# The stepwise inversion of 16x16 diagonal blocks in VectorE's queue instead of GpSimd's, in a two-model forward pass

## The chip, the cores and the metric
The kernel runs on one core of a Trainium2 chip. Its time is the device time of that core in microseconds (us). Before the change it is 3070.37 us, the median of 3 runs (3067.53 to 3080.65). Engines are named as the profile names them: PE is TensorE's matrix multiply, PEld its weight load, DVE is VectorE, ACT is ScalarE, POOL is GpSimd, SP is SyncE, whose queue (SPq) issues most DMAs.

## The reference, cut to what matters
Two networks run one after the other on 512 tokens of width 1024. The first has two layers, and each layer has two gated feed-forward blocks around a mixing block. The mixing block joins three mixers: attention over selected keys (8 heads), an RWKV-7 recurrence (4 heads) and a gated delta rule (4 heads). The second network has one layer with two more mixers, cross attention and a mixture of 16 experts; the change does not touch it.

RWKV-7 and the gated delta rule are both solved in chunks of 64 tokens. Each chunk needs the solution of a unit lower triangular system:

```
lower = where(strict, einsum('bhncd,bhnsd->bhncs', kb, k) * decay, 0.0)
sol = triangular_solve(eye(C) + lower, rhs, left_side=True, lower=True, unit_diagonal=True)
```

The kernel computes the result of both recurrences with the same code, which it calls the delta mixers. For each block of 128 tokens (two chunks, 8 heads in all) it inverts the 16x16 blocks on the diagonal of these systems exactly, in 15 steps of elimination, and treats what lies outside these blocks by three rounds of substitution with matrix products.

## The kernel before, in words
**Stages.** In each of the two layers of the first network there is a stage, here the delta stage, in which the attention of the layer and both delta mixers run interleaved. It works on four blocks of 128 tokens, numbered 0 to 3. For one block the work is:
- `rwkv_front` and `gdn_front` (from line 1132, `delta_fronts`) make products on TensorE and write the system's matrix into a tile `low` (name in the code: `L`). The last TensorE instructions for it are four transposes of the tile `gsq`, in the rows `bank<-consts,gsq`, and ScalarE copies them into `low`.
- `delta_inverses` (line 672) sends the 16x16 diagonal blocks of `low` through DRAM into the tile `LL` of 64 rows, 8 DMAs out (`lows<-low`) and one back (`LL<-lows`). POOL masks `low` (one instruction, `low<-low,consts`). Then come the steps: in step j a product of two broadcast views is written into a scratch third of `LL` and subtracted from the inverse, which is another third; 15 steps of two instructions, each 64 rows by 15 to 64 elements. One DMA takes the inverse out (`inverses<-LL`), and 8 bring it into the tile `DD` (`DD<-inverses`). The two tiles `DD0` and `DD1` take turns.
- `delta_solve` (line 704) begins with TensorE products of `DD` and `low`, then of the right-hand sides, for RWKV (`rrh`) and for the gated delta rule (`grh`), and then makes the rounds of substitution (`Y`).
- `delta_states` carries the states `S` through the chunks, and `dsa_attend` makes the attention's scores (`kz,qT`), softmax (`sm`) and values (`po`), also in four blocks, of growing length.

A block's front may be built when the fronts before it are done and the solves are no more than two blocks back.

**What sets the order.** The streams above are Python generators. `weave` (line 310) advances one of them at a time, the first whose operands are ready. Whether they are ready is told by a ledger in the program: `account` (line 2192) enters each instruction with a cost from a small table and keeps a clock for each engine:

```
if self.name == "POOL":
    return n * 2.1 + 220
return n / 0.96 + (200 if any(isinstance(x, bass.AP) for x in args[2:3]) and len(args) == 4 or "accum_out" in kw else 150)
```

The last line is VectorE's. When no stream is ready, the time until the next one is, in this ledger, is filled with small matmuls of a constant, `bank<-mean`, one for 234 ns (line 262):

```
n, self.idle = int(self.idle / 234), 0.0
for _ in range(n):
    self.t.matmul(p[:, :128], self.mean, self.mean, start=True, stop=True)
```

They compute nothing that is used; in this text they are called fillers. Afterwards a scheduler of the framework sets the order in each engine's own queue. Each engine then executes its queue strictly in that order and waits at semaphores. All engine instructions pass through the helper at line 2184, so the profile shows that line for nearly all of them, and they are told apart by the names of their tiles.

Of the kernel before, what the change touches and what calls it, by code (L numbers as in the profile page):

```python
# [14 lines left out]
OP = mybir.AluOpType  # L15
# [185 lines left out]
class Net:  # L201
# [470 lines left out]
    def delta_inverses(self, pool, l, f):  # L672

        g = self.g
        DD = [self.tl(pool, [128, 8, 128], f"DD{i}", 1) for i in range(2)]
        for d in DD:
            g.memset(d, 0.0)
        for b in range(NB):
            yield lambda: min(f["front"]) > b and min(f["back"]) > b - 2  # L680
            L, D, low, inv = f["L", b], DD[b % 2], self.lows[l * NB + b], self.inverses[l * NB + b]
            for k in range(8):
                at = slice(16 * k, 16 * k + 16)
                self.move(low[k].rearrange("q s t -> s q t"), L[at, :, at])
            W = self.tl(pool, [64, 3, 256], "LL", 1)
            g.memset(W[:, 1], 0.0)
            g.memset(W[:, 1, ::17], 1.0)
            self.move(W[:, 0], low.rearrange("k q s t -> (k q) (s t)"))

            N, X, t = (W[:, i].rearrange("p (i c) -> p i c", i=16) for i in range(3))  # L690
            for j in range(15):
                c, n = j + 1, 15 - j
                g.tensor_tensor(t[:, :c, :n], N[:, None, j + 1:, j].to_broadcast([64, c, n]),
                                X[:, :c, j, None].to_broadcast([64, c, n]), op=OP.mult)
                g.tensor_tensor(X[:, :c, j + 1:], X[:, :c, j + 1:], t[:, :c, :n], op=OP.subtract)
            self.move(inv.rearrange("k q s t -> (k q) (s t)"), W[:, 1])
            for k in range(8):
                at = slice(16 * k, 16 * k + 16)
                self.move(D[at, :, at], inv[k].rearrange("q s t -> s q t"))
            g.tensor_tensor(L, L, self.c("off16")[:, None, :].to_broadcast([128, 8, 128]), op=OP.mult)  # L700
            f["DD", b] = D
            f["D"] = b + 1
# [1654 lines left out]
```

## Time and profile before
| | |
|---|---|
| median of 3 runs | 3070.37 us |
| profiled execution, its own time | 3068.61 us |
| its span, first to last instruction | 3066.7 us |
| mean granted TensorE clock | 0.982 |
| PE busy / DVE busy / ACT busy / POOL busy | 2967.5 / 1779.5 / 1314.9 / 491.1 us |
| delta stage, first layer, from its first product with `DD` to its end | 614.16 to 764.90 us |
| the same in the second layer | 1776.6 to 1929.0 us |

The kernel is bound by TensorE nearly everywhere. The chip's profile counts an engine busy while an instruction is in it; fillers count as busy too. The time that an engine stood still before an instruction is told in square brackets behind a row, with the instruction or DMA that ended the wait. Names are those of the program's tiles, with buffer numbers left out in the trace and kept in the order below.

### The profile page before, as it was taken

Reading aid. Unit: us, or ns where it says so; the run is one execution under the profiler, and the core shown is the slowest. Engines: PE = TensorE matmul, PEld = TensorE weight load, DVE = VectorE, ACT = ScalarE, POOL = GpSimd, SP = SyncE. Lnnn points to the kernel's source line nnn. Section 1 sums busy time; section 2 is a strip of 40 time slices with the busy share of each in tenths; the row PEclk is TensorE's granted clock in tenths of the full one; section 3 lists DMA queues with packets and bytes.
Section 4 is the critical chain, followed back from the end, with each engine's and each line's share of the span. In section 5 each row is a group of like instructions: output and inputs, shape, how many; then the busy total and the mean of one; then the engine's idle time right before and its main releaser. Section 6 shows DMA issues by size and latency. Waiting matters only on the chain. (4 is left out here: it accounts for less than half of the span.)

```text
span 3066.7 us, 40239 instructions
## 1 busy us (share of the span) xinstructions
PE 2967.5 (97%) x15422; PEld 2366.7 (77%) x15422; DVE 1779.5 (58%) x2969; ACT 1314.9 (43%) x2117; POOL 491.1 (16%) x674
## 2 busy tenths in 40 slices
PE   9999999999999999999998999999999999989997
PEld 7888866786888888888866786888887777767775
DVE  5343559574544445444559675543445657649988
ACT  3222444544322234222344445422225455558886
POOL 1000144431000000000044431000001000026532
PEclk9999999999999999999999899999999999999999
DMA  4333322001333333333322000333333312759993
GB/s 133 100 96 100 120 76 76 18 15 33 108 98 96 96 91 102 96 96 96 119 83 72 24 17 14 124 97 97 99 94 114 99 49 63 289 172 375 388 385 142
DMA packets 129529, 349.95 MB, mean 114 GB/s; under 512 B 30400, under 2 KB 37456, under 8 KB 129200
## 3 DMA queue, kind: packets, MB, share of 16 engines
q1 hardware_dynamic: 120608, 325.17, 32.4%
q0 software_dynamic: 3648, 12.85, 1.3%
q10 hardware_dynamic: 5072, 9.27, 0.8%
q8 instruction: 123, 2.02, 0.3%
q14 instruction: 78, 0.64, 0.1%
HBM read 325.28 MB, written 21.95 MB: 113 GB/s over the span
## 5 line engine op out<-in xcount | busy, mean ns | idle before, releaser
L2184 ACT ACTIVATE wh<-w 128x1024 fp32r<-128x1024 f32 (+2 forms) x386 | 400.1, 1037 | 1115.4 <-PE bank L2184 790.7
L2184 PE MATMUL bank<-hh,wl 128*128 128x512 f32 x2000 | 783.5, 392 | 16.7 <-POOL wl L2184 9.7
L2184 PE MATMUL bank<-hh,wh 128*128 128x512 f32 x2000 | 790.5, 396 | 0.7 <-ACT hh L2184 0.6
L2184 PE MATMUL bank<-hl,wh 128*128 128x512 f32 x2000 | 782.5, 391 | 3.2 <-DVE hl L2184 3.1
L2184 PEld LDWEIGHTS bank<-hh,wl 128*128 128x128 f32 x2000 | 377.2, 189 | 101.8 <-POOL wl L2184 14.1
L2184 PEld LDWEIGHTS bank<-hh,wh 128*128 128x128 f32 x2000 | 376.8, 188 | 91.4 <-issue 13.0
L2184 PEld LDWEIGHTS bank<-hl,wh 128*128 128x128 f32 x2000 | 377.2, 189 | 86.4 <-DVE hl L2184 6.8
L2184 DVE TENSOR_TENSOR wl<-w,wh 128x1024 fp32r<-128x1024 f32 (+1 forms) x334 | 399.5, 1197 | 74.1 <-ACT wh L2184 57.3
L2184 PE MATMUL bank<-ul,wh 128*128 128x512 f32 x704 | 274.3, 390 | 0.0
L2184 PE MATMUL bank<-uh,wl 128*128 128x512 f32 x704 | 273.9, 389 | 0.0
L2184 PE MATMUL bank<-uh,wh 128*128 128x512 f32 x704 | 273.2, 389 | 0.0
L2184 DVE TENSOR_TENSOR hl<-w,hh 128x1024 fp32r<-128x1024 f32 x192 | 238.3, 1265 | 21.2 <-ACT hh L2184 15.1
L2184 DVE TENSOR_TENSOR u<-bank,rfeat 128x512 f32<-128x512 f32 x88 | 60.8, 691 | 279.0 <-PE bank L2184 279.0
L2184 ACT ACTIVATE hh<-w 128x1024 fp32r<-128x1024 f32 x192 | 201.4, 1059 | 45.0 <-PE bank L2184 45.0
L2184 DVE SCALAR_TENSOR_TENSOR x<-bank,x 128x512 f32<-128x512 f32 x96 | 66.4, 692 | 241.2 <-PE bank L2184 241.2
L2184 POOL COPY cosi<-consts 128x128 f32<-128x128 f32 x4 | 2.2, 557 | 1079.5 <-ACT sg L2184 1079.5
L2184 DVE TENSOR_TENSOR g<-bank,rfeat 128x512 f32<-128x512 f32 x88 | 60.9, 692 | 186.6 <-PE bank L2184 185.8
L2184 PEld LDWEIGHTS bank<-ul,wh 128*128 128x128 f32 x704 | 132.2, 188 | 28.7 <-DVE ul L2184 1.3
L2184 PEld LDWEIGHTS bank<-uh,wh 128*128 128x128 f32 x704 | 132.2, 188 | 27.4
L2184 PEld LDWEIGHTS bank<-uh,wl 128*128 128x128 f32 x704 | 132.2, 188 | 27.2
L2184 POOL TENSOR_TENSOR wl<-w,wh 128x1024 fp32r<-128x1024 f32 (+1 forms) x52 | 122.1, 2348 | 186.3 <-ACT wh L2184 176.0
L2184 PE MATMUL bank<-hh,exh 128*96 128x512 f32 (+1 forms) x272 | 109.3, 403 | 0.0
(574 smaller groups left out, 4619.4 us busy)
## 6 DMA issues: line engine op xcount, KB each, us to landing
w<-in_wgu SPq DMA_DIRECT2D x176, 512.0 KB, 3.5
w<-in_wd SPq DMA_DIRECT2D x64, 512.0 KB, 3.6
w<-in_w_eg SPq DMA_DIRECT2D x64, 512.0 KB, 6.8
w<-in_w_eu SPq DMA_DIRECT2D x64, 512.0 KB, 6.3
w<-in_w_ed SPq DMA_DIRECT2D x62, 512.0 KB, 8.2
w<-in_wd SPq DMA_DIRECT2D x32, 384.0 KB, 3.1
w<-in_w_o SPq DMA_DIRECT2D x20, 512.0 KB, 4.1
w<-in_w_gd SPq DMA_DIRECT2D x16, 512.0 KB, 3.5
```

The costliest lines, as they stand in the source:

```text
L2184: r = f(*args, **kw)
```

## The change
Two lines of the loop over the 15 steps name another engine: `self.v`, VectorE, where `g`, POOL, stood. The clearing of the tiles and the mask of `low` stay on POOL. The formulas and the tiles are the same.

```
             for j in range(15):
                 c, n = j + 1, 15 - j
-                g.tensor_tensor(t[:, :c, :n], N[:, None, j + 1:, j].to_broadcast([64, c, n]),
-                                X[:, :c, j, None].to_broadcast([64, c, n]), op=OP.mult)
-                g.tensor_tensor(X[:, :c, j + 1:], X[:, :c, j + 1:], t[:, :c, :n], op=OP.subtract)
+                self.v.tensor_tensor(t[:, :c, :n], N[:, None, j + 1:, j].to_broadcast([64, c, n]),
+                                     X[:, :c, j, None].to_broadcast([64, c, n]), op=OP.mult)
+                self.v.tensor_tensor(X[:, :c, j + 1:], X[:, :c, j + 1:], t[:, :c, :n], op=OP.subtract)
             self.move(inv.rearrange("k q s t -> (k q) (s t)"), W[:, 1])
```

Since the ledger charges the steps to VectorE, the order of instructions changes too, in the two delta stages and nowhere else. TensorE, first layer, where the fillers stand ahead of block 1's products (- is before, + is now; `kz` and `qT` are attention, `rE2` belongs to RWKV):

```order
 L2184 MATMUL bank_793_4442<-kz_439_2583,qT_432_2576 128x128
 L2184 MATMUL bank_794_4443<-kz_439_2583,qT_432_2576 128x128
-L2184 MATMUL bank_799_4454<-mean_67 128x128 x6
+L2184 MATMUL bank_799_4454<-mean_67 128x128 x31
 L2184 MATMUL bank_799_4454<-rE2_745_4280,consts_8_100 128x256
```

There were 6 fillers and there are 31. In the whole stage of one layer there were 59 and there are 118.

TensorE a little further on, before: the products of block 1's matrix, then its transposes to tokens, and in the last row the transposes of `gsq`, which complete block 1's `low`.

```order
L2184 MATMUL bank_804_4473<-rE0_744_4279,rkk_747_4282 128x128 x2
L2184 MATMUL bank_804_4473<-rR_425_2569,rE0_744_4279 128x128 x2
L2184 MATMUL bank_805_4480<-rkk_747_4282,rcs_743_4278 128x128 x2
L2184 MATMUL bank_805_4480<-rR_425_2569,rcs_743_4278 128x128 x2
L2184 MATMUL bank_806_4487<-rkk_747_4282,rcs_743_4278 128x128 x2
L2184 MATMUL bank_806_4487<-rR_425_2569,rcs_743_4278 128x128 x2
L2184 MATMUL bank_808_4495<-consts_8_100,rV_426_2570 128x128 x2
L2184 MATMUL bank_808_4495<-consts_8_100,rkk_747_4282 128x128 x2
L2184 MATMUL bank_809_4502<-consts_8_100,rE3_746_4281 128x128 x2
L2184 MATMUL bank_809_4502<-consts_8_100,rA_424_2568 128x128 x2
L2184 MATMUL bank_810_4509<-consts_8_100,gsq_775_4378 128x128 x4
```

TensorE at the same place now (`DD0_716` holds block 0's inverse, `low_720` is block 0's matrix; the first two products with `DD0_716` stand just ahead of these):

```order
L2184 MATMUL bank_810_4532<-consts_8_100,rV_426_2570 128x128 x2
L2184 MATMUL bank_810_4532<-consts_8_100,rkk_747_4282 128x128 x2
L2184 MATMUL bank_811_4539<-DD0_716_4130,low_720_4138 128x128 x4
L2184 MATMUL bank_812_4545<-grh_736_4207,DD0_716_4130 128x128 x4
L2184 MATMUL bank_813_4551<-consts_8_100,rE3_746_4281 128x128 x2
L2184 MATMUL bank_813_4551<-consts_8_100,rA_424_2568 128x128 x2
L2184 MATMUL bank_814_4558<-rrh_728_4170,low_720_4138 128x128 x4
L2184 MATMUL bank_815_4564<-grh_736_4207,low_720_4138 128x128 x4
L2184 MATMUL bank_816_4570<-rV_426_2570,ak_800_4488 128x64 x4
L2184 MATMUL bank_817_4576<-Y0_738_4216,low_720_4138 128x128 x4
L2184 MATMUL bank_818_4582<-Y1_742_4277,low_720_4138 128x128 x4
L2184 MATMUL bank_819_4588<-consts_8_100,gsq_775_4378 128x128 x4
```

Before, the transposes of `gsq_775` stood 19 rows ahead of the first product with block 0's inverse; now they stand 13 rows behind it. Block 2's moved in the same way behind block 1's inverse; block 3's stood behind block 2's inverse already.

VectorE, block 1 of the first layer, before: preparing block 2's RWKV operands, one for one with the decay tile `DT` of the gated delta rule.

```order
L2184 TENSOR_TENSOR rE3_820_4590<-rK_422_2566,rE3_820_4590 128x256
L2184 SCALAR_TENSOR_TENSOR DT_847_4681<-bank_848_4682,gb_479_2776,consts1_9_102 128x128
L2184 TENSOR_TENSOR rK_422_2566<-rK_422_2566,cols_63 128x2x128
L2184 SCALAR_TENSOR_TENSOR DT_847_4681<-bank_848_4682,gb_479_2776,consts1_9_102 128x128
L2184 TENSOR_TENSOR rE2_819_4589<-rR_425_2569,rK_422_2566 128x256
```

VectorE at the same place now, with the steps of block 1 (`LL_820`) between:

```order
L2184 SCALAR_TENSOR_TENSOR DT_839_4719<-bank_840_4720,gb_479_2776,consts1_9_102 128x128
L2184 TENSOR_TENSOR LL_820_4603<-LL_820_4603 64x15
L2184 TENSOR_TENSOR rE2_825_4661<-rR_425_2569,rK_422_2566 128x256
L2184 TENSOR_TENSOR LL_820_4603<-LL_820_4603 64x15
L2184 SCALAR_TENSOR_TENSOR DT_839_4719<-bank_840_4720,gb_479_2776,consts1_9_102 128x128
L2184 TENSOR_TENSOR LL_820_4603<-LL_820_4603 64x2x14
L2184 TENSOR_TENSOR rR_425_2569<-rR_425_2569,rW_423_2567 128x2x128
L2184 TENSOR_TENSOR LL_820_4603<-LL_820_4603 64x2x14
```

Each of the 30 instructions of a block's chain needs the one before it. Between them stand other instructions: 21 in block 0, 29 in block 1, 30 in block 2 and 5 in block 3 (an instruction and the read of its accumulator counted as one).

## Rows read from the trace of the kernel before
**Rows 1.** The page: busy us, share of the span, instructions.
```profile
PE 2967.5 (97%) x15422; PEld 2366.7 (77%) x15422; DVE 1779.5 (58%) x2969; ACT 1314.9 (43%) x2117; POOL 491.1 (16%) x674
```
**Rows 2.** Stretches of the delta stage; first layer, then all of the second.
```profile
core 0: us, PE busy (x) PEld busy (x) DVE busy (x) ACT busy (x) POOL busy (x), PEclk, DMA share, GB/s
614.16:639.43 25.27, 23.91 (x204) 21.18 (x205) 21.88 (x57) 13.43 (x35) 12.87 (x33) 1.00 0.08 12
639.43:665.91 26.48, 26.35 (x275) 22.80 (x275) 18.97 (x58) 8.91 (x20) 12.32 (x33) 0.94 0.10 16
665.91:718.13 52.22, 47.23 (x530) 36.76 (x529) 29.94 (x92) 25.79 (x69) 12.14 (x32) 0.97 0.09 24
718.13:764.90 46.77, 44.96 (x400) 35.82 (x400) 20.40 (x50) 21.83 (x48) 0.00 (x0) 0.88 0.08 24
1776.60:1929.00 152.40, 143.47 (x1410) 117.58 (x1411) 91.28 (x255) 71.26 (x173) 37.23 (x98) 0.94 0.09 22
```
**Rows 3.** Timeline of TensorE, first layer: start, us, operation, count, [idle before <-releaser].
```profile
584.80 0.61 PE L2184 MATMUL bank<-consts,gsq 128*128 128x128 f32 x4
...
614.16 1.13 PE L2184 MATMUL bank<-DD,low 128*128 128x128 f32 x8 [0.70 <-DMA lows<-low]
...
639.43 1.40 PE L2184 MATMUL bank<-DD,low 128*128 128x128 f32 x8 [1.27 <-DMA DD<-inverses]
...
665.91 1.06 PE L2184 MATMUL bank<-DD,low 128*128 128x128 f32 x8
...
718.13 2.05 PE L2184 MATMUL bank<-DD,low 128*128 128x128 f32 x8 [4.55 <-DMA DD<-inverses]
719.97 1.92 PE L2184 MATMUL bank<-rrh,DD 128*128 128x128 f32 x8
...
761.53 3.62 PE L2184 MATMUL bank<-mean 128*128 128x128 f32 x30
```
**Rows 4.** Timeline of POOL, first layer: the mask and the steps, blocks 0 and 1.
```profile
591.93 2.35 POOL L2184 TENSOR_TENSOR low<-low,consts 128x1024 f32<-128x1024 f32 x1 [18.63 <-ACT PT L2184]
594.25 12.46 POOL L2184 TENSOR_TENSOR LL<-LL 64x15 f32<-64x15 f32 x30
...
619.81 12.38 POOL L2184 TENSOR_TENSOR LL<-LL 64x15 f32<-64x15 f32 x30
```
**Rows 5.** Timeline of SyncE's DMA queue, first layer, blocks 0 and 1.
```profile
586.06 4.36 SPq L668 DMA_DIRECT2D lows<-low  x8
...
612.46 3.68 SPq L668 DMA_DIRECT2D lows<-low  x8
```
**Rows 6.** Timeline of VectorE, first layer.
```profile
577.22 1.12 DVE L2184 SCALAR_TENSOR_TENSOR DT<-bank,gb,consts 128x128 f32<-128x128 f32 x4
...
586.17 0.16 DVE L2184 COPY wc<-rW 128x4 f32<-128x4 f32 x1
586.24 0.35 DVE L2184 CUSTOM_DVE_ANT_0 sm<-bank,consts,ssq 128x128 f32<-128x128 f32 x1
...
592.07 2.50 DVE L2184 TENSOR_TENSOR rkk<-rkk,rcs 128x256 f32<-128x256 f32 x1
...
596.17 0.47 DVE L2184 TENSOR_TENSOR rcs<-rK,rE 128x256 f32<-128x256 f32 x1
...
624.72 0.74 DVE L2184 SCALAR_TENSOR_TENSOR rb<-bank,consts 128x256 f32<-128x256 f32 x2
```
**Rows 7.** VectorE's groups by form, small shapes: count | busy us, mean ns of one.
```profile
L2184 DVE SCALAR_TENSOR_TENSOR gsp<-gsp,gsp 128x16 f32<-128x16 f32 x18 | 3.2, 175 | 0.6
L2184 DVE TENSOR_TENSOR M<-oe,oe 128x64 f32<-128x64 f32 x1 | 0.2, 218 | 0.0
```

## The prediction
> **What bounds the kernel now.** I read the busy table of the page first. TensorE is busy for 97% of the span, VectorE for 58%, GpSimd (POOL) for 16% [rows 1]. So time is won or lost where TensorE waits, or where it does something that is no work. Next I read TensorE's timeline inside the delta stage of a layer, which is the only place where the order of instructions differs between the two kernels. In it I looked for the four places at which TensorE first multiplies with an inverted block, `bank<-DD,low`: 614.16, 639.43, 665.91 and 718.13 us [rows 3]. These four points and the stage's end, where the output projection starts at 764.90, cut the stage into four stretches of 25.27, 26.48, 52.22 and 46.77 us [rows 2]. In the second layer the same five points span 152.40 us, against 150.7 in the first [rows 2], so one layer is worked out and doubled. TensorE waits 0.70 us before the first point, 1.27 before the second, nothing before the third, and 4.55 before the fourth [rows 3].
>
> What paces the first three points is a loop through several queues. When TensorE has made the last half of a block's matrix (the transposes `bank<-consts,gsq`), ScalarE copies it, and SyncE sends 8 DMAs (`lows<-low`) and one back. POOL then does the 30 steps, SyncE sends the inverse out and 8 DMAs back into `DD`, and TensorE can go on. The pieces: from the transposes at 584.80 [rows 3] to the first DMA at 586.06 [rows 5] 1.3 us; from the first DMA at 612.46 [rows 5] to the first step at 619.81 [rows 4] 7.4 us; 30 steps 12.4 us [rows 4]; from the end of the steps (594.25 + 12.46 = 606.71) [rows 4] to the product at 614.16 [rows 3] 7.45 us. The loop therefore costs 28.5 us per block, and 12.4 of them are the step that is moved. Before the change it hardly shows: in TensorE's queue the transposes of blocks 1 and 2 stand ahead of the previous block's `DD`, so two blocks are on the way at once.
>
> **The change, part by part.** Removed from POOL: 240 instructions, 30 in each of 8 blocks, 12.4 us a block [rows 4]. That in itself is worth nothing, since POOL waits for most of the stage. The mask of the matrix stays on POOL: 2.35 us at 591.93 [rows 4], and a VectorE instruction that falls into it still takes 2.50 us instead of 0.4 [rows 6].
>
> Added to VectorE: the same 240. The trace before has no VectorE step of this form, so I bound it. From above: 0.175 us with 16 elements and 0.218 with 64 [rows 7], 0.2 on average, if each step is charged whole; 30 make 6 us. From below: a 4-element copy is followed by the next start after 0.07 us (586.17 to 586.24) [rows 6]; 30 make 2.1 us. Where a step stands between other instructions I take 0.12 us, 3.6 us a block, since it has 15 to 64 elements and a 128-element instruction starts 0.26 us after its neighbour (four in 1.12 us) [rows 6]. Where steps follow each other I take 0.2.
>
> But the steps do not stand alone. In VectorE's order the chains of blocks 0, 1 and 2 alternate with other instructions, one for one: 21, 29 and 30 of them. Those start 0.33 us apart with 256 elements [rows 6], 0.26 with 128, and I take 0.6 with 512. So block 1's chain lasts 15 x 0.33 + 10 x 0.26 + 4 x 0.25 + 3.6 = 12.2 us, with waits for TensorE some 13; block 2's 21 x 0.33 + 4 x 0.6 + 4 x 0.26 + 3.6 = 14. Block 0's starts behind the instruction at 596.17 [rows 6], lasts 16 x 0.33 + 4 x 0.26 + 3.6 = 10, and near its end waits for a product behind the long row of filler matmuls; it ends near 607.7, a us later than on POOL. Only block 3 has five others, 7 us. So in three of four blocks the loop gets nothing shorter.
>
> The second effect weighs more: TensorE's order changes, because the ledger that writes it charges the steps to another engine. (1) The filler matmuls (`bank<-mean`) in the stage go from 59 to 118 per layer. Thirty records, that is 15 fillers, take 3.62 us [rows 3], 0.24 each, so 59 more cost 14.2 us of TensorE. (2) The transposes of blocks 1 and 2 now stand behind the previous block's `DD`, so the loop can no longer run ahead. (3) Attention's third block moves behind the last `DD`.
>
> To price the stretches I counted the columns streamed in each, a transpose's as half: before, 13,568, 14,592, 28,672 and 22,720; now 18,432, 13,760, 21,696 and 30,336. The stretches of before, less their waits (0.7 in the last, estimated) and less 0.24 us for each of the 0, 0, 6 and 27 fillers, come to 24.0, 26.5, 46.2 and 39.6 us: 1.71 ns a column. Fillers are now 0, 0, 30 and 42.
>
> Sum for one layer:
> - To the first `DD`: its chain ends 1 us later, +1.0. TensorE waits there with 10 us of work queued behind, which moves into later stretches.
> - First to second `DD`: 5,120 columns to the transposes (8.8 us), a slow start after the wait 1.0, then 1.3 + 7.4 + 13 + 7.45 = 39.0; TensorE's own 31.5 fit inside. Against 25.3: +13.7.
> - Second to third: 3,072 columns (5.3), 1.0 + 1.3 + 7.4 + 14 + 7.45 = 36.5. Against 26.5: +10.0.
> - Third to fourth: TensorE is longer, 37.1 for its columns, 7.2 for 30 fillers and 1.0 = 45.3; the loop ends at 19.0 + 1.0 + 1.3 + 7.4 + 7 + 7.45 = 43.2. Against 52.2: -6.9.
> - Fourth to the end: 51.9 + 42 x 0.24 + 1.0 = 63.0. Against 46.8: +16.2.
>
> Together +34.0 us, twice +68.0. The slow start is an estimate: after the wait of 4.55 us the first two groups took 2.05 and 1.92 us [rows 3], where the same group took 1.06 at 665.91 [rows 3], and the granted clock of that last stretch is 0.88, a mean of its two levels of 1.2 and 2.4 GHz [rows 2]; so it costs up to 1.9 us, and I take half. The profiled execution took 3068.61 us, 1.9 beyond its span and 1.8 below the median of the runs. 3068.6 + 68.0 = 3136.6; I say 3136.
>
> What queues behind the added waits: VectorE's queue blocks at the first step of each block until its DMA has landed, with the operands of TensorE's next products behind it; TensorE waits for `DD` with all else behind it.
>
> On how the steps add up, the row shows 256-element instructions of 0.41 us starting 0.33 apart (two in 0.74) [rows 6]. The Trainium skill (VectorE: DVE Perf Modes, "The DRAIN you can't avoid") says that the next instruction does not start until the pipe is empty, and advises to keep the number of instructions low; this speaks against 240 small ones on the busier engine. By it block 1's chain would be about 3.6 us longer and the time some 3150; by the row the overlap is there, and the sum goes by the row.
>
> **The rivals.**
> *Faster: only the steps count.* The chain of 30 runs on VectorE in 6 us instead of 12.4, so each loop is 6 us shorter, and the waits before `DD` (0.70 + 1.27 + 4.55 = 6.5 us) [rows 3] go, with 1.9 of slow start: -8.4 a layer, 3052 us. For it: 0.2 us a step against 0.41 on POOL [rows 4, 7]. Against it: the alternation and the order of TensorE. It decides if block 1's first step starts before 622 us of the span instead of near 634. The Trainium skill (GPSIMD Engine Reference, section 4.1) has this rule: two-input elementwise work belongs on VectorE, GpSimd being about twice slower; the rows agree on one step alone. Chance 0.04.
> *Fillers only.* All waits at `DD` are hidden: the stretches cost 31.5, 23.5, 44.3 and 62.0 us, together +10.5 a layer, 3090 us. For it: nothing that the trace shows hides 7 to 13 us there. Against it: the loop without its steps alone is 16 us. Chance 0.12.
> *Heavier.* The interleaved instructions wait for TensorE in turn, and the chains of blocks 1 and 2 take 6 us more each: +12 a layer, 3160 us. For it: many of them read a `bank`. Against it: those products are mostly done when the chain starts late. Chance 0.20.
> *No change*, since the transfers and not the steps pace the loop: 3070 us, chance 0.04.
>
> **How the numbers follow.** My forecast holds 0.60. The range reaches from the fillers-only case to the heavier one: 3091 to 3160 us. A measurement of this kernel tells 0.5%, 15 us, from no change. Slower by more than that are the forecast, the heavier case and most of fillers-only: 0.89. Within it lie the no-change case and a remainder of fillers-only: 0.07. Faster: 0.04.
>
> **What would show it.** TensorE's waits for `DMA DD<-inverses` should be 4 to 7, 5 to 9 and 10 to 15 us before the first three `DD` of a layer and near none before the fourth, the reverse of before. The stage should last some 34 us longer per layer, the rest of the span the same. VectorE's busy time should grow by 25 to 48 us, POOL's fall by about 99. The chain on VectorE should last 10 to 16 us in blocks 0 to 2 and 7 in block 3. I am wrong if the first step of block 1 starts as early as before, or if TensorE stands still less in the stage than it does now.

## The result, and the profile after

The changed kernel takes 3146.47 us (median of 4 runs, 3145.57 to 3150.33), the kernel before 3068.95 (4 runs). The ratio is 1.0259, with a 95% interval of 1.0238 to 1.028. The forecast was 3136 us in a range of 3091 to 3160. The profiled execution took 3147.16 us with a span of 3145.4: 78.7 us more than the span of before. The busy table of the changed kernel, against [rows 1]:

```profile
PE 3005.5 (96%) x15658; PEld 2409.1 (77%) x15658; DVE 1820.0 (58%) x3209; ACT 1316.8 (42%) x2117; POOL 414.9 (13%) x434
```

VectorE's busy time grew by 40.5 us and POOL's fell by 76.2. Next the stretches of the delta stage, cut at the same four products as in [rows 2]; the last row is the second layer from its first product with `DD` to the stage's end. The columns are those of [rows 2].

```profile
615.03:662.70 47.67, 39.86 (x336) 34.29 (x337) 29.08 (x97) 15.77 (x41) 2.96 (x3) 0.75 0.04 7
662.70:706.42 43.72, 30.91 (x198) 26.97 (x198) 26.90 (x91) 14.62 (x38) 2.76 (x3) 0.73 0.08 19
706.42:751.85 45.43, 41.99 (x497) 36.35 (x498) 26.29 (x95) 17.01 (x44) 2.87 (x2) 0.94 0.09 19
751.85:807.85 56.00, 55.40 (x514) 44.48 (x515) 26.94 (x72) 31.32 (x76) 0.00 (x0) 0.97 0.08 23
...
1815.81:2006.36 190.55, 167.25 (x1545) 141.51 (x1545) 110.24 (x356) 80.19 (x201) 9.09 (x8) 0.86 0.08 18
```

The first two stretches grew by 22.4 and 17.2 us, the third shrank by 6.8, the last grew by 9.2; together 42.1. TensorE's granted clock in the first two is 0.75 and 0.73, where it was 1.00 and 0.94. TensorE's timeline of the first layer shows the places that [rows 3] show of before:

```profile
598.44 7.16 PE L2184 MATMUL bank<-mean 128*128 128x128 f32 x62 [0.80 <-DVE LL L2184]
...
615.03 2.04 PE L2184 MATMUL bank<-DD,low 128*128 128x128 f32 x8 [6.25 <-DMA DD<-inverses]
...
626.37 0.60 PE L2184 MATMUL bank<-consts,gsq 128*128 128x128 f32 x4
...
662.70 2.05 PE L2184 MATMUL bank<-DD,low 128*128 128x128 f32 x8 [5.66 <-DMA DD<-inverses]
...
670.48 0.61 PE L2184 MATMUL bank<-consts,gsq 128*128 128x128 f32 x4
...
706.42 2.05 PE L2184 MATMUL bank<-DD,low 128*128 128x128 f32 x8 [9.83 <-DMA DD<-inverses]
...
726.42 0.61 PE L2184 MATMUL bank<-consts,gsq 128*128 128x128 f32 x4
...
751.85 1.13 PE L2184 MATMUL bank<-DD,low 128*128 128x128 f32 x8 [3.43 <-DMA DD<-inverses]
```

The `gsq` rows are the transposes that complete a block's matrix; they now follow the previous block's product, and the next product waits for the inverse. What the loop consists of is seen for block 1 first in SyncE's DMA queue, which answers to [rows 5]:

```profile
627.63 3.63 SPq L668 DMA_DIRECT2D lows<-low  x8
632.49 0.47 SPq L668 DMA_DIRECT2D LL<-lows  x1
654.33 0.46 SPq L668 DMA_DIRECT2D inverses<-LL  x1
657.45 3.62 SPq L668 DMA_DIRECT2D DD<-inverses  x8
```

VectorE's timeline between these DMAs:

```profile
632.83 2.58 DVE L2184 SCALAR_TENSOR_TENSOR gQ<-gQ,gsq 128x256 f32<-128x256 f32 x1
...
637.93 0.16 DVE L2184 TENSOR_TENSOR LL<-LL 64x15 f32<-64x15 f32 x1
638.01 0.41 DVE L2184 TENSOR_TENSOR rE<-rR,rK 128x256 f32<-128x256 f32 x1
638.35 0.16 DVE L2184 TENSOR_TENSOR LL<-LL 64x15 f32<-64x15 f32 x1
...
646.28 0.42 DVE L2184 SCALAR_TENSOR_TENSOR ak<-bank,consts 128x256 f32<-128x256 f32 x1 [0.98 <-PE bank L2184]
...
654.08 0.17 DVE L2184 TENSOR_TENSOR LL<-LL 64x15 f32<-64x15 f32 x1
```

The first step starts 10.3 us behind the first DMA, because VectorE has other work in front of it. The chain then takes 16.3 us, since every second instruction is another one, and some of those wait for TensorE or ScalarE.

### The profile page after: what moved, and what is told of

It is laid out like the page before. It is cut to its first block, busy times and chain, and to the rows that moved or that the text cites. A ratio compares the mean times of both kernels' runs of the same rounds, so it can differ in the third digit from the quotient of the medians.

```text
span 3145.4 us, 40718 instructions
## 1 busy us (share of the span) xinstructions
PE 3005.5 (96%) x15658; PEld 2409.1 (77%) x15658; DVE 1820.0 (58%) x3209; ACT 1316.8 (42%) x2117; POOL 414.9 (13%) x434
## 5 line engine op out<-in xcount | busy, mean ns | idle before, releaser
L2184 ACT ACTIVATE hh<-w 128x1024 fp32r<-128x1024 f32 x192 | 201.3, 1059 | 45.3 <-PE bank L2184 45.1
```

The source lines that it names most:

```text
L2184: r = f(*args, **kw)
```

## The experiments

All ratios are to the kernel before, run on the same chip beside them.

**Order and engine apart.** The helper runs a step on one engine and books it on another in the ledger, so the four combinations can be had. In e1 the steps run on VectorE and TensorE keeps its order of before; in e2 they run on POOL and TensorE has the order of after.

```
+def _step(does, pays):
+    def call(*args, **kw):
+        does.eng.tensor_tensor(*args, **kw)
+        pays.account(args, kw, list(args))
...
-                self.v.tensor_tensor(X[:, :c, j + 1:], X[:, :c, j + 1:], t[:, :c, :n], op=OP.subtract)
+                _step(self.v, self.g)(X[:, :c, j + 1:], X[:, :c, j + 1:], t[:, :c, :n], op=OP.subtract)
```

(e1; in e2 it is `_step(self.g, self.v)`, and the product of each step is edited alike.)

> The 240 steps run on VectorE, but the ledger books them on POOL, so TensorE keeps the order of before (59 fillers per layer, the transposes of blocks 1 and 2 ahead of the previous block's first product with DD). Theory A, the order costs: 3060 to 3085 us, because VectorE's interleaved chains end about when POOL's did and nothing is put behind them on TensorE; waits of TensorE for the inverses at the first three points under 4 us each. Theory B, the engine costs (VectorE's queue is blocked by the steps and the steps by the queue): 3110 to 3150 us, with waits of 4 us and more at the first three points.

> The 240 steps run on POOL as before, but the ledger books them on VectorE, so TensorE has the order of after (118 fillers per layer, the transposes behind). Theory A: 3120 to 3140 us, a little under after, since POOL's chain starts as soon as its DMA has landed (7.4 us behind the first DMA instead of 10.3) and lasts 12.4 us instead of 16; the second and third stretch about 40 and 37 us instead of 47.7 and 43.7. Theory B: 3070 to 3090 us.

Measured: e1 3100.85 us, ratio 1.0101 (1.0077 to 1.0124); e2 3118.12 us, 1.0172 (1.0147 to 1.0197). Neither theory alone holds: e1 lies between its two ranges, e2 2 us below the first of its own. The engine costs 1.0%, the order 1.7%, and their sum, 2.7%, is about the 2.6% of the change.

In e1 little of the cost is a late inverse. TensorE's waits for the inverse in the first layer's stage of before, from 584 to 765 us: us in total, times, longest.

```profile
PE bank L2184 <- DMA DD<-inverses: 5.8, 2, 4.5
```

The same of e1, from 584 to 778 us:

```profile
PE bank L2184 <- DMA DD<-inverses: 8.5, 2, 6.5
```

That is 2.7 us of the 12.3 by which e1's stage is longer, from the first transposes to its end. TensorE's other waits grew by 4.6 us, and its rows took 5.0 more, with the granted clock at 0.93 where it was 0.95. In e2 the steps are back on POOL. TensorE's timeline still shows waits for the inverse: smaller ones than after's at the first three products, a larger one at the fourth.

```profile
612.73 2.04 PE L2184 MATMUL bank<-DD,low 128*128 128x128 f32 x8 [5.72 <-DMA DD<-inverses]
...
654.95 1.05 PE L2184 MATMUL bank<-DD,low 128*128 128x128 f32 x8
...
689.37 1.74 PE L2184 MATMUL bank<-DD,low 128*128 128x128 f32 x8 [3.72 <-DMA DD<-inverses]
...
736.48 2.04 PE L2184 MATMUL bank<-DD,low 128*128 128x128 f32 x8 [6.24 <-DMA DD<-inverses]
```

**The fillers.** e3 is the kernel after, with the stage's fillers booked in the ledger and not issued.

```
-            self.t.matmul(p[:, :128], self.mean, self.mean, start=True, stop=True)
+            (_ledger_only(self.t) if getattr(self, "mute", 0) else self.t.matmul)(p[:, :128], self.mean, self.mean, start=True, stop=True)
```

> The kernel after, with the same ledger, but the 118 fillers per layer of the delta stage booked and not issued. If every filler costs its 0.24 us: 28 us a layer less, about 3090 us. If only those cost that stand where TensorE does not wait soon after (the last stretch, 43 of them): 10 us a layer less, about 3126 us. If they only keep the clock up: no less than 3146 us, with a lower granted clock.

Measured: 3158.92 us, ratio 1.0303 (1.0278 to 1.0327), 12 us slower than with them: the third case of the expectation. The intervals of the two ratios just touch, but the fastest of the four executions of e3 (3157.50) is slower than the slowest of after (3150.33). The kernel after, up to its first product with `DD`:

```profile
560.00:615.03 55.03, 46.29 (x359) 40.67 (x359) 43.58 (x140) 23.53 (x64) 13.18 (x17) 0.92 0.04 6
```

Four stretches of e3: up to the first product, the last two of the first layer's stage, and 60 us behind the second layer's stage.

```profile
560.00:616.43 56.43, 41.66 (x267) 34.87 (x266) 42.27 (x140) 23.26 (x64) 13.21 (x17) 0.71 0.04 6
...
704.79:755.23 50.44, 37.98 (x438) 31.25 (x438) 26.55 (x95) 17.14 (x44) 2.52 (x2) 0.84 0.08 17
755.23:808.91 53.68, 48.60 (x430) 36.25 (x431) 26.27 (x72) 30.99 (x76) 0.00 (x0) 0.94 0.03 10
...
2011.47:2071.47 60.00, 58.53 (x243) 47.48 (x243) 31.91 (x41) 21.37 (x27) 0.00 (x0) 0.95 0.42 141
```

The granted clock fell from 0.92 to 0.71 ahead of the first product and from 0.94 to 0.84 in the third stretch, which got 5 us longer. The last stretch lost 42 fillers, 10 us by their duration, and got only 2.3 us shorter: without them TensorE stands still for 5.1 us there (0.6 with them), and the granted clock is 0.94 instead of 0.97. Of the 12 us, some 5 lie in the two stages. Another 6.9 lie behind the second one, where both kernels have the same instructions: the granted clock of the last row, 0.95, is 1.00 in the 60 us behind that stage of after.

**The transposes' place.** e9 is the kernel after, but a solve of block 0 or 1 waits in the program for the next block's front.

```
-        yield lambda: f["D"] > b
+        yield lambda: f["D"] > b and (b > 1 or min(f["front"]) > b + 1)
```

> As after, but the solve of blocks 0 and 1 waits in the program until the next block's front is built, so the transposes of blocks 1 and 2 stand ahead of the previous block's first product with DD again, as before the change; the steps still alternate on VectorE and the ledger still books them there (the row of 31 fillers stays). If the transposes' place is what the new order costs: 3095 to 3110 us, the level of e1. If the fillers or the place of attention's third block cost: 3125 to 3150 us.

Measured: 3093.31 us, ratio 1.0073 (1.0057 to 1.0088), 53 us less than after and 2 us below the first range of the expectation, with the row of 31 fillers still there. TensorE's timeline of e9; the wait for the inverse before the second product is gone:

```profile
609.18 0.60 PE L2184 MATMUL bank<-consts,gsq 128*128 128x128 f32 x4
614.66 1.37 PE L2184 MATMUL bank<-DD,low 128*128 128x128 f32 x8 [2.79 <-DMA lows<-low]
...
649.13 0.46 PE L2184 MATMUL bank<-DD,low 128*128 128x128 f32 x2 [0.24 <-ACT low L2184]
```

The edit moves more than the transposes: the scores of attention's second block and part of those of its third stand further ahead too. But of the 29.9 us by which e9's first stage is shorter than that of after, 23.0 lie ahead of the third product, and attention's third block stands behind that product in both.

**The alternation on VectorE.** e5 is e1, and e7 is the kernel after, with the steps of a block together in VectorE's queue: an instruction traced behind them goes behind the last step if the ledger has it start no earlier than the first (SHIFT = 0).

```
+def _behind(eng, ins, start):
+    if getattr(eng, "last", None) is not None and eng.net.together and start >= eng.first + SHIFT:
+        eng.net.tc.add_manual_dep(ins, eng.last.name, mybir.DependencyInfo(
+            mybir.DependencyClass.NoSync, mybir.DependencyReason.DATA), reason="steps together")
```

> As e1 (steps on VectorE, order of before on TensorE), but the 30 steps of a block stand together in VectorE's queue: what is traced behind them, and is not due earlier by the ledger, is queued behind the last step. Theory I, the alternation is what makes VectorE dear: the chain falls from 13 to 18 us to 6 to 7, the first three points come no later than before, the wait before the fourth falls under 2 us: 3045 to 3068 us. Theory Q, the queue behind the steps is what costs (TensorE waits for operands that VectorE now makes 6 us later): 3080 to 3100 us, with TensorE waiting for VectorE's tiles.

> As after (ledger and TensorE's order), but the 30 steps of a block stand together in VectorE's queue. Theory I: the loop gets about 9 us shorter in blocks 1 and 2, stretches of 38 and 35 us instead of 47.7 and 43.7; 3100 to 3118 us, no more than e2. Theory Q: 3135 to 3150 us.

Measured: e5 3097.17 us, ratio 1.009 (1.0075 to 1.0106), no measurable gain over e1 and in the range of theory Q; e7 3131.82 us, 1.0207 (1.0192 to 1.0223), 15 us less than after and between its two ranges. Theory I falls for the order of before: the chain is indeed down to 7.4 us, and TensorE waits for no inverse, but for other tiles of VectorE instead. Block 0's chain in VectorE's timeline of e5 (line 2363 is the helper's):

```profile
594.14 7.40 DVE L2363 TENSOR_TENSOR LL<-LL 64x15 f32<-64x15 f32 x30 [2.01 <-DMA LL<-lows]
```

TensorE's waits in e5 from 585 to 785 us: who waits for what, us in total, times, longest.

```profile
PE bank L2184 <- DVE S L2184: 7.0, 2, 6.8
PE bank L2184 <- DVE gqk L2184: 5.7, 1, 5.7
PE bank L2184 <- DVE rE L2184: 5.2, 2, 4.6
PE bank L2184 <- DVE Y L2184: 4.6, 1, 4.6
```

In e7 TensorE waits for no inverse in this stage either, but for 24 us for three tiles of VectorE; the longest, in the same columns:

```profile
PE bank L2184 <- DVE mn L2184: 10.6, 2, 8.0
```

So a block's steps cost VectorE's queue time that TensorE sees in one form or the other. Together they make other operands late. Alternating they make the inverse late in the order of after, and in the order of before (e1) both, other operands more than the inverse.

**The last block alone.** In e4, e6 and e13 only block 3's steps are on VectorE, in TensorE's order of before: alternating, together, and together behind what is due within 1 us of the first step.

```
-                g.tensor_tensor(X[:, :c, j + 1:], X[:, :c, j + 1:], t[:, :c, :n], op=OP.subtract)
+                _step(self.v if b == 3 else g, g)(X[:, :c, j + 1:], X[:, :c, j + 1:], t[:, :c, :n], op=OP.subtract)
```

(e4; e6 and e13 have `_behind` besides, with a SHIFT of 0 and of 1000 ns.)

> Only block 3's steps run on VectorE, the ledger books all on POOL, TensorE's order is that of before row for row. If the steps of the last block bind there: its chain falls from 11.9 to about 7 us, the wait of 4.55 us before the fourth product goes together with up to 1.9 us of slow start: 4.5 to 6.4 us a layer, 3056 to 3060 us. If VectorE's queue holds the chain up: 3066 to 3072 us, with the wait still there.

> As e4 (only block 3 on VectorE), but its 30 steps stand together in VectorE's queue. Theory I: the chain falls from 12.3 us (e4) to 6 to 7, the wait of 6.4 us before the fourth product goes and 1.9 us of slow start with it: 3053 to 3062 us. Theory Q: attention's instructions, 6 us later, take the place of the wait: 3066 to 3076 us.

> As e6 (block 3's steps together on VectorE, the rest on POOL), but the instructions that the ledger has due up to 1 us behind the first step go ahead of it, the recurrence's state S among them, for which TensorE waited 6.9 us in e6. If VectorE's queue has room there: 3050 to 3060 us. If the softmax instructions that now stand behind the steps make the next wait: 3062 to 3070 us, with TensorE waiting some 5 us for sm.

Measured: e4 3072.80 us, ratio 1.0022 (1.0008 to 1.0036), slightly slower; e6 3063.92, 0.9991 (0.9981 to 1.0001); e13 3063.82, 0.9989 (0.9977 to 1.0). Neither e6 nor e13 can be told from the kernel before. In e4 the chain starts behind softmax work and alternates with it, and in TensorE's timeline the wait before the fourth product grew from 4.55 us [rows 3] (the profiled execution took 3083.05 us, the longest of twelve):

```profile
720.26 2.05 PE L2184 MATMUL bank<-DD,low 128*128 128x128 f32 x8 [6.44 <-DMA DD<-inverses]
```

In e6 that wait is gone, and one for the state S stands in its place. TensorE's longest wait of e6 in the first layer's stage:

```profile
PE bank L2184 <- DVE S L2184: 7.1, 2, 6.9
```

In e13 the longest is one for Y, where the expectation had `sm`:

```profile
PE bank L2184 <- DVE Y L2184: 4.8, 1, 4.8
```

**Steps on POOL, booked dearer.** If the order counts, the ledger can make a better one. In the kernel before, each step is booked at 413, 700 and 800 ns.

```
-        n = max(int(np.prod(x.shape[1:])) for x in aps)
+        n = max(int(np.prod(x.shape[1:])) for x in aps) if not getattr(self, "fixed", 0) else (self.fixed - 220) / 2.1
...
+        pays.fixed = 413
+        pays.account(args, kw, list(args))
```

(e10; 700 in e11 and 800 in e12.)

> The kernel before, steps on POOL, but the ledger books each step at the 413 ns that POOL takes for it (12.4 us for 30) instead of by its formula (some 260 to 350). In the order that comes of it block 2's transposes stand 27 rows behind block 1's first product with DD; block 1's stand ahead as before. If the transposes' place is what an order costs: TensorE waits 5 to 10 us before the third point and none more before the second; 3085 to 3105 us. If a truer ledger makes a better order: 3050 to 3068 us.

> As the last, but each step booked at 700 ns, far above what it takes: all transposes stand ahead of the previous block's first product, block 3's too (38 rows ahead of block 2's), and 30 fillers per layer are left of 59. If the transposes' place decides: no wait for the inverses over 1 us at any of the four points, 3045 to 3062 us. If fillers are needed for the clock: a granted clock under 0.975 and 3066 to 3085 us.

> As the last, each step booked at 800 ns: block 3's transposes stand 55 rows ahead of block 2's first product, and a dozen fillers per layer are left in the stage. The transposes' place: 3045 to 3062 us, as the kernel booked at 700. The clock: slower than that one by 5 to 20 us, with a granted clock lower by 0.003 or more.

Measured: e10 3058.57 us, ratio 0.9971 (0.9956 to 0.9985); e11 3058.99, 0.9971 (0.9959 to 0.9982); e12 3052.22, 0.9946 (0.9928 to 0.9964). e12 beats both kernels, and all three beat the one before. For e10 my expectation was wrong in sign: block 2's transposes do stand behind block 1's product, and the kernel is faster. I had counted rows; its timeline counts time:

```profile
640.39 1.13 PE L2184 MATMUL bank<-DD,low 128*128 128x128 f32 x8 [2.56 <-DMA DD<-inverses]
...
653.13 0.60 PE L2184 MATMUL bank<-consts,gsq 128*128 128x128 f32 x4
...
690.68 1.16 PE L2184 MATMUL bank<-DD,low 128*128 128x128 f32 x8
```

Between block 2's transposes and its product TensorE had 37.6 us of other rows, 3.6 of them a wait for VectorE, and no wait for the inverse. e12 goes further, 59.5 us for block 2 and 48.9 for block 3, with no wait for an inverse in the whole stage:

```profile
643.97 0.60 PE L2184 MATMUL bank<-consts,gsq 128*128 128x128 f32 x4
...
686.32 0.60 PE L2184 MATMUL bank<-consts,gsq 128*128 128x128 f32 x4
...
703.50 1.16 PE L2184 MATMUL bank<-DD,low 128*128 128x128 f32 x8
...
735.25 1.16 PE L2184 MATMUL bank<-DD,low 128*128 128x128 f32 x8
```

e11 has no wait for an inverse in its two stages either. It keeps 55 of the 60 fillers that the trace of before has in the first stage from its first transposes on, so little of the 8.8 us that it gains can be theirs. In the two stages of before TensorE waited 11.4 us for the inverse. e12 keeps 35, 9 of 34 behind the first product, and its clock hardly suffered: 0.981 over the whole run, 0.982 before. No run tells how much of its lead over e11 comes from the fewer fillers.

So the rule that these runs fit is not "transposes ahead" but: TensorE waits for the inverse by what the loop takes beyond the time that its own rows fill between a block's transposes and that block's product. In the first layer, us from transposes to product, with the wait for the inverse in it:

| | block 1 | block 2 | block 3 |
|---|---|---|---|
| before | 34.2, wait 1.3 | 33.4, none | 28.9, wait 4.6 |
| after | 36.3, wait 5.7 | 35.9, wait 9.8 | 25.4, wait 3.4 |
| e1 (VectorE, order of before) | 38.0, none | 38.3, none | 31.6, wait 6.5 |
| e2 (POOL, order of after) | 30.7, none | 29.2, wait 3.7 | 28.2, wait 6.2 |
| e9 (VectorE, solve held back) | 40.0, none | 35.4, none | 27.2, wait 4.4 |
| e12 (POOL, booked at 800) | 64.9, none | 59.5, none | 48.9, none |

Where TensorE waited, the time in the table is the loop's own. Where it did not, the loop can be read to the end of the eight `DD<-inverses`, and some 1.4 to 1.9 us more, which the rows with a wait show from there to the product: 27 to 38 us, less than the table's time in each of these blocks.

Before the change, block 1's loop took 34.2 us and not the 28.5 of the prediction. Its first DMA, at 612.46 [rows 5], came 7.2 us behind the transposes instead of 1.3: in SyncE's queue it stands right behind the DMAs that bring block 0's inverse.

```profile
608.72 3.64 SPq L668 DMA_DIRECT2D DD<-inverses  x8
```

So two blocks on the way at once hold each other up in that queue.

## Why the prediction was right, and which of its terms were not

**Right: the mechanism and its places.** Waits of 6.25, 5.66 and 9.83 us for `DMA DD<-inverses` came before the first three products, where 4 to 7, 5 to 9 and 10 to 15 had been given; in the second layer 6.41, 4.20 and 10.02. Before the fourth, near none had been given, and it was 3.43 and 3.44. VectorE's busy time grew by 40.5 us (25 to 48 given). e2 shows that the order costs more than the engine, as the prediction has it, and e9 that most of the order's price goes when the transposes, point (2), stand ahead again. What the engine costs in the order of before, 1.0% (e1), is no term of the sum, which priced how the steps delay the inverse and not how they delay VectorE's other tiles. e5 shows that this price remains without the alternation.

**Stretch by stretch, first layer.** To the first product: +1.0 forecast, +0.9 measured. First to second: 39.0 forecast, 47.7 measured. The loop's pieces there are 11.3 us to the transposes (9.8 forecast), 1.3 to the first DMA (1.3), 10.3 to the first step (7.4), 16.3 for the chain (13) and 8.5 from there to the product (7.45). Second to third: 36.5 forecast, 43.7 measured, by 7.8 (6.3), 1.4 (1.3), 9.9 (7.4), 17.0 (14) and 7.6 (7.45). Third to fourth: 45.3 forecast, 45.4 measured, and that is luck. The forecast had TensorE's own rows as the longer path, with the loop done at 43.2. Measured, TensorE's part is 42.0 and the loop ends last: 20.0 us to the transposes (20.0 forecast), 1.3 (1.3), 9.0 (7.4), 8.0 (7) and 7.2 (7.45). Fourth to the end: 63.0 forecast, 56.0 measured.

**Mis-sized: how late the chain starts and how long it lasts.** The 7.4 us to the first step were POOL's, which had only the mask in front of the steps. VectorE has its queue of operands there: 2.9 and 2.5 us more. The prediction had named that queueing, on the other side ("VectorE's queue blocks at the first step"), and had not priced it here. The chain took 3 us more than forecast in blocks 1 and 2 (16.3 and 17.0 us, where 10 to 16 had been given), because instructions between the steps wait for TensorE or ScalarE, by 0.70, 0.45, 0.98 and 0.92 us in block 1; behind a wait of 1.89 us TensorE's granted clock is 0.50, the lower of its two levels, from 638.48 to 650.14 (rows of 1.22 us at 639.63 where the same four take 0.71 at 605.96). That was the heavier rival's mechanism at half its size.

**Wrong: the fillers as a price.** The sum charged each at 0.24 us in the last stretch, 10.1 us. e3 shows 2.3 us there, and a loss when all are taken away. This is the step that failed in kind: a filler's duration is not its price. In the trace of after the 42 fillers do take their 10 us, since TensorE stands still for only 0.6 us of that stretch; the other rows took 45.3 us there, where 1.71 ns a column had given 51.9. By luck the error hid that of the loop: 15.9 us too little in the first two stretches, 7.0 too much in the last.

**The two layers.** They were forecast as alike, +34 each. The first gave 43.0. In the second, the stage from its first product grew by 39.2 and the way from the transposes to that product by 1.0 (by TensorE's rows the stage of before goes from 1776.48 to 1927.80, 151.3 us; the 152.4 of [rows 2] reach 1.2 us into the output projection), but 4.65 us came back between the stages, where the instructions are the same. The windows show where: the same rows of TensorE ahead of the second layer's products, first of before.

```profile
1737.60:1748.00 10.40, 10.40 (x67) 9.72 (x68) 5.88 (x17) 4.18 (x12) 0.00 (x0) 0.59 0.01 2
```

The same of after:

```profile
1779.80:1786.40 6.60, 6.60 (x68) 6.20 (x69) 5.17 (x16) 4.27 (x12) 0.00 (x0) 1.00 0.01 2
```

At the full clock after, mostly at the half before, 3.8 us apart. No run here shows why the clock fell there in one and not in the other; it is no effect of a step of the sum. All in all +78.7 us instead of +68.

**POOL's busy time** fell by 76 us, not 99: the 12.4 us of a row of 30 steps [rows 4] hold the gaps between them.

**The rivals.** Faster fell: the first step of block 1 starts at 637.93 us, not before 622. No change fell. Fillers only fell with e3 and with the waits at the products.

## What to carry to other kernels

The price of moving work to a faster engine is what that engine's queue already carries for the others: with the steps of all four blocks VectorE's queue gave back more than the faster steps saved, alternating or together (e1, e5), and with those of the fourth alone about as much (e4, e6, e13). Where a program's own ledger writes the order, a change of engine is a change of order, and the two are told apart by running the work on one engine and booking it on the other. For a loop through other queues, count the time of TensorE's rows between the last product that feeds the loop and the first that needs its result, in us and not in rows; where it covers the loop, few fillers will do (e12 has 9 behind its first product).

## What the runs showed of the hardware

- Dependent neighbours on VectorE do not overlap, independent ones do. Thirty steps together took 7.40 us, 0.25 each, and were busy for 6.40 of them; alternating, a step put only 0.08 to 0.17 us into the queue (637.93 to 638.01). The Trainium skill (VectorE: DVE Perf Modes, "The DRAIN you can't avoid") has the next operation wait until the pipe is empty, and adds that one that is not held starts earlier: the steps together agree with the first, the alternating ones with the second. The prediction had named the first alone. The alternation is thus cheap for the queue and dear for the chain.
- While POOL masks the matrix (2.54 us from 632.59), VectorE's `gQ` took 2.58 us instead of 0.42; it ended 2.5 us ahead of the first step. The Trainium skill (SBUF — State Buffer, "SBUF: two separate sides") says that the two engines share a port pair under an exclusive lock; the row agrees. No run took the mask away, so its share in the late start is not known.
- Taking matmuls away made the kernel slower by 12 us (e3), with the clock of the whole run down from 0.971 to 0.960, and more than half of that behind the stages that they were taken from.
